# A two-block transformer kernel: four modulation blocks moved from the first routing into the second layer's mixing, the entry's loads reordered and paired, and the expert loads' queue bound to program order

## The chip, the cores and the metric

The kernel runs on one core of a Trainium2 chip. The metric is the device time of one execution in microseconds (us). The kernel before takes 2650.71 us, the median of three runs (2647.95 to 2651.56). The execution that was profiled took 2657.17 us, of which the trace spans 2655.0 us.

Engines are called PE (matrix engine; PEld is its weight load), DVE (vector), ACT (scalar), POOL (GpSimd) and SP (the queue from which nearly all loads are issued; SPq in the trace).

## The reference

A first block of two layers, then a second block. One layer of the first block works on 512 tokens `x` and 256 context tokens `xc`:

```
mods  = silu(c) @ ada_w[i] + ada_b[i]           # 1024 x 6144, split in six: shift, scale, gate, twice
cmods = silu(c_ctx) @ ada_w[i] + ada_b[i]
h  = rms_norm(x, n1) * (1 + sc1) + sh1          # hc the same from xc
a_b, a_c, a_h, b_v, b_g, c_q, c_k, c_v, d_q, d_k, d_v = split_proj(h @ w_in)
x  = x + g1 * (concat(conv a, conv b, window attention c, global attention d) @ w_out)
h2 = rms_norm(x, n2) * (1 + sc2) + sh2
aff = softmax(h2 @ router);  gates, idx = top_k(aff.T, cap)     # 16 experts choose their tokens
y  = (silu(xs @ w_gate[e]) * (xs @ w_up[e])) @ w_down[e]        # for each expert, 1024 x 1024 weights
x  = x + g2 * scatter_add(idx, gates * y)
```

In the second layer only `x` goes on (64 tokens for each expert; in the first layer 64 of `x` and 32 of `xc`). The second block (gated delta rule, dilated attention and a gated feed-forward) isn't touched by the change. Everything is float32; the dense products split weights and activations in a high and a low part.

## The kernel before, in words

The stages follow one another: entry (token loads, their norm sums, the first modulation blocks), the first layer's mixing, its routing, its 16 experts, the same for the second layer, then the second block. Each engine executes its instructions in one order, which is fixed when the program is built: a scheduler places them, and each engine waits on semaphores where data or a buffer isn't ready. SP is such a queue too: a load that waits for its buffer holds up every load behind it.

**Buffers for weights.** `raw_tile` (L187) takes one of the five 512 KB buffers of the pool `wp` (tile `raw`). They serve everything in turn: the columns of `w_in` and `w_out` (`colload`, L487, `colload2`, L493), the quarters of the modulation blocks (`ada_load`, L196) and, in the experts, five of the 25 buffers through which the expert weights rotate. The others there are 18 of `rawA` and 2 of `rawB` (in the second layer 20 and 8). `wload` (L1055) loads one tile of 128 x 1024 after the other, in the order in which PE uses them: g0, u0, g1, d0, u1, g2, d1, ... d15, eight tiles each, 384 in a layer; tile i goes to slot i % 25, where slots 18 to 22 are the five `raw`. A tile's buffer is free again when PE has read it (L1243 for `x`, L1248 for `xc`; in the second layer L1237).

**Modulation.** `ada_gen` (L309) makes a block of 512 modulation columns from four quarter tiles: 16 matrix products (L318), a copy on ACT (L323), four transposes (L327), a sum and a bias on DVE (L329, L330). After the products of a block it may already load the first three quarters of the next one (L320). In the first layer's mixing it makes blocks 4 to 11 of layer 0 and 0 to 7 of layer 1. After block 7 of layer 1 the line

```
if 3 < b < 11 or (l == 1 and b != 7 and b < 11):
    ada_load(l, b + 1, hfs=range(4 if l == 1 and b > 7 else 3))
```

holds by its first half, so the first three quarters of block 8 of layer 1 are loaded there. Blocks 8 to 11 of layer 1 are made in the first layer's routing (L1090, with `steps(ga, 2)` at L1120 and L1152).

**Entry.** Small rows of vectors, the tokens and eight quarters of blocks are issued in turn by SP. The unit `c_q` takes two strips of 64 columns (`pre0[1]`, L272). All four blocks 0, 2, 1, 3 of layer 0 are made before the norm of the tokens (`norm1_first`, L385: for eight column tiles k the high part `hh` on ACT, L396, and the low part `hl` on DVE and POOL, L397, L398). `dense` (L420) runs the units of `w_in`: `wh` on ACT (L442), `wl` on POOL (L443), then 24 products (L473, L475).

**Routing.** Router logits (L1095), softmax (Exp at L1107), eight rounds of top-8 on DVE (L1146 to L1149), the normalised tokens to memory (`hd`, L1132), zeros to the two tables of sums (L1138), a gather of each expert's tokens (L1209), their transposes (L1221), and the first expert's products (L1243).

Of the kernel before, what the change touches and what calls it, by code (L numbers as in the profile page):

```python
# [10 lines left out]
F32 = mybir.dt.float32  # L11
# [123 lines left out]
def main_kernel(ctx, tc, I, out, stop=None, dbg=None, manual=False):  # L135
# [37 lines left out]
    dx = pool(ctx, "dx", space=DRAM).tile([128, 8 * 768], F32)  # L173
# [44 lines left out]
    rows = ent.tile([128, 4, 128], F32)  # L218
    xin = xip.tile([128, 4, 1024], F32)
    cin = xip.tile([128, 2, 1024], F32)  # L220
    ada0 = ent.tile([128, 4, 4, 1024], F32)
# [20 lines left out]
    x_load(1)  # L242
    row_load(G, 0, "qn", I["q_norm_g"], 2, dup=True)
    row_load(G, 0, "kn", I["k_norm_g"], 2, dup=True)
    row_load(G, 0, "cbb", I["conv_b_b"].rearrange("l (h p) -> (l h) p", p=128), 4)
    row_load(G, 0, "lng", I["conv_ln_g"].rearrange("l (h p) -> (l h) p", p=128), 4)
    row_load(G, 0, "lnb", I["conv_ln_b"].rearrange("l (h p) -> (l h) p", p=128), 4)
# [3 lines left out]
    x_load(2)  # L251
    SY.dma_start(sinkb, bass.AP(tensor=I["sink"].tensor, offset=I["sink"].offset, ap=[[0, 128], [1, 8]]))
    row_load(SY, 0, "fg", I["final_g"].rearrange("(k p) -> k p", p=128), 8)
    row_load(SY, 0, "ln1", I["ln1_2"].rearrange("l (k p) -> (l k) p", p=128), 8)
    x_load(3)
# [6 lines left out]
    ada_load(0, 0, ada0[:, 0], hfs=(2, 3))  # L262
    ada_load(0, 2, ada0[:, 2])
    for t in range(2):
        SY.dma_start(cin[:, t, :], I["ctx"][0, t * 128:(t + 1) * 128, :])
    ada_load(0, 1, ada0[:, 1])
    pre0 = {}
    pre0[0] = raw_tile().rearrange("p (k c) -> p k c", k=8)
    SY.dma_start(pre0[0], I["w_in"][0, :, 1536:1664].rearrange("(k p) c -> p k c", p=128))
    pre0[1] = raw_tile().rearrange("p (k c) -> p k c", k=8)  # L270
# [3 lines left out]
    ada_load(0, 3, ada0[:, 3])  # L274
# [34 lines left out]
    def ada_gen(l, blocks, pl, psp):  # L309
        g, o, n = RO["adab"]  # L310
        for b in blocks:
# [8 lines left out]
            if 3 < b < 11 or (l == 1 and b != 7 and b < 11):  # L320
                ada_load(l, b + 1, hfs=range(4 if l == 1 and b > 7 else 3))
# [10 lines left out]
            yield  # L332

# [7 lines left out]
    if True:  # L341
        with ExitStack() as e0:
# [4 lines left out]
            def rows_to_cols(g, n):  # L347
                p = pse.tile([128, 512], F32, name="rc")
                T.transpose(p[:, :n], rows[0:n, g, :], ident[0:n, 0:n])
                V.tensor_copy(cols[:, g, 0:n], p[:, :n])  # L350

            rows_to_cols(0, 16)
            A.activation(s2[:, :, 0], col("c"), AF.Silu)
            A.activation(s2[:, :, 1], col("cc"), AF.Silu)
            ga = ada_gen(0, (0, 2, 1, 3), sqp, pse)
            ss = ent.tile([128, 6], F32)
            for t in range(6):
# [16 lines left out]
                if t == 1:  # L374
                    rows_to_cols(1, RO["n", 1])
# [4 lines left out]
            for g in (0, 2, 3):  # L380
                rows_to_cols(g, RO["n", g])
            V.tensor_scalar(nsink, sinkb, -1.0, None, op0=OP.mult)

        entry.close()

        def norm1_first(sqp):
            a1 = sqp.tile([128, 8, 2], F32, name="a1")
            for k in range(8):
# [32 lines left out]
        def dense(units, hh, hl, dw, dps, la=3, pre={}, ahead=None):  # L421
# [5 lines left out]
            def load(i):  # L427
                if i in pre:
                    raw[i] = pre[i]
                elif i < len(units):  # L430
                    raw[i] = raw_tile().rearrange("p (k c) -> p k c", k=8)
                    units[i][0](raw[i])

            def split(i):
                if i < len(units):
                    nk = units[i][4] if len(units[i]) > 3 else 8
                    hi[i] = []
                    for a in range(0, nk, 4):
# [3 lines left out]
                        A.activation(wh[:, :n], raw[i][:, a:a + n], AF.Copy)  # L442
                        G.tensor_tensor(wl[:, :n], raw[i][:, a:a + n], wh[:, :n].bitcast(F32), op=OP.subtract)  # L443
# [41 lines left out]
        def colload(src, c0, n=128):  # L485
            def f(raw):
                SY.dma_start(raw[:, :, 0:n], src[:, c0:c0 + n].rearrange("(k p) c -> p k c", p=128))  # L487
            return f

        def colload2(src, ca, cb):  # L490
            def f(raw):
                for h, c in enumerate((ca, cb)):
# [529 lines left out]
        def experts(l, rwpA, lg, rbias, a2, nA, nB):  # L1022
# [37 lines left out]
            if has:  # L1060
                ada_load(1, 8)
# [918 lines left out]
```

## Time and profile before

| stage | from, us | to, us |
|---|---|---|
| entry, to the first full pace of the units | 0 | 65 |
| first layer's mixing | 65 | 456 |
| its routing | 456 | 502 |
| its experts | 502 | 1057 |
| second layer's norm, mixing and routing | 1057 | 1389 |
| its experts | 1389 | 1868 |
| second block | 1868 | 2655 |

| | us |
|---|---|
| median of three runs | 2650.71 |
| profiled execution | 2657.17 |
| its span in the trace | 2655.0 |
| PE busy | 2476.4 (93%) |
| DVE, ACT, POOL busy | 1092.9, 870.2, 637.8 |

The span is the time from the first to the last instruction of the trace. PE is busy nearly all of the time, so a stage ends when PE is through with it, save where PE waits: in the entry, in routing, and in parts of the second layer. In the experts' stages the DMA engines are busy throughout as well.

### The profile page before, as it was taken

Reading aid. Unit: us, or ns where it says so; the run is one execution under the profiler, and the core shown is the slowest. Engines: PE = TensorE matmul, PEld = TensorE weight load, DVE = VectorE, ACT = ScalarE, POOL = GpSimd, SP = SyncE. Lnnn points to the kernel's source line nnn. Section 1 sums busy time; section 2 is a strip of 40 time slices with the busy share of each in tenths; the row PEclk is TensorE's granted clock in tenths of the full one; section 3 lists DMA queues with packets and bytes.
Section 4 is the critical chain, followed back from the end, with each engine's and each line's share of the span. In section 5 each row is a group of like instructions: output and inputs, shape, how many; then the busy total and the mean of one; then the engine's idle time right before and its main releaser. Section 6 shows DMA issues by size and latency. Waiting matters only on the chain.

```text
span 2655.0 us, 41308 instructions
## 1 busy us (share of the span) xinstructions
PE 2476.4 (93%) x16415; PEld 1500.4 (57%) x16415; DVE 1092.9 (41%) x2371; ACT 870.2 (33%) x1769; POOL 637.8 (24%) x552
## 2 busy tenths in 40 slices
PE   7999999699999999899979989898899999999998
PEld 4766777344444333577753322132577787888886
DVE  4488852311111113689641102021665555444411
ACT  4544362211111110464531111110562435443422
POOL 3533112011111100633220000000333233444443
PEclk8999999899999999799989999999899999999999
DMA  8454455999999998222179999999421102333332
GB/s 281 140 165 139 149 177 197 322 383 385 385 386 385 388 394 313 58 59 52 61 289 386 394 398 399 399 404 409 130 67 32 40 25 64 95 96 96 92 96 67
DMA packets 324758, 584.08 MB, mean 220 GB/s; under 512 B 36864, under 2 KB 190007, under 8 KB 323927
## 3 DMA queue, kind: packets, MB, share of 16 engines
q1 hardware_dynamic: 311943, 555.16, 57.7%
q0 software_dynamic: 12480, 26.23, 4.1%
q8 instruction: 129, 2.11, 0.3%
q14 instruction: 62, 0.51, 0.1%
q10 hardware_dynamic: 144, 0.08, 0.0%
HBM read 556.74 MB, written 18.87 MB: 217 GB/s over the span
## 4 chain that ended last, share of the span: by engine, by line
PE 62%; DMA 21%; DVE 9%; issue 3%; POOL 2%; ACT 1%; SPq 1%; ACTq 0%; DVEq 0%; POOLq 0%
PE px L473 21%; DMA rawA<-in_w_gate_dram 4%; DMA rawA<-in_w_down_dram 4%; PE ax L1243 3%; DMA rawA<-in_w_up_dram 3%; PE yx L1243 3%; PE ux L1243 3%; PE g L473 2%; PE s L553 2%; PE y L584 2%; PE px L475 2%; DMA rawB<-in_w_gate_dram 2%; PE pt L565 2%; PE ac L1248 2%; PE pt L473 2%
## 5 line engine op out<-in xcount | busy, mean ns | idle before, releaser
L443 POOL TENSOR_TENSOR wl<-raw,wh 128x512 fp32r<-128x512 f32 (+1 forms) x312 | 408.2, 1311 | 962.0 <-ACT wh L442 768.1
L442 ACT ACTIVATE wh<-raw 128x512 fp32r<-128x512 f32 (+1 forms) x312 | 193.6, 625 | 441.2 <-PE px L473 211.0
L473 PE MATMUL px<-hh,wh 128*128 128x512 f32 x768 | 315.7, 412 | 6.4 <-DVE xT L1401 1.8
L473 PE MATMUL px<-hh,wl 128*128 128x512 f32 x768 | 313.1, 408 | 6.6 <-POOL wl L443 6.6
L473 PE MATMUL px<-hl,wh 128*128 128x512 f32 x768 | 314.6, 410 | 3.8 <-DVE hl L1019 1.9
L1225 ACT ACTIVATE xt<-tr,mod,a 128x64 f32<-128x64 f32 x256 | 86.9, 405 | 295.5 <-PE tr L1221 285.1
L473 PEld LDWEIGHTS px<-hh,wh 128*128 128x128 f32 x768 | 148.7, 194 | 41.2 <-issue 6.1
L473 PEld LDWEIGHTS px<-hh,wl 128*128 128x128 f32 x768 | 148.8, 194 | 39.7 <-POOL wl L443 7.3
L473 PEld LDWEIGHTS px<-hl,wh 128*128 128x128 f32 x768 | 148.7, 194 | 37.5 <-issue 3.8
L1369 DVE SCALAR_TENSOR_TENSOR Yx<-yx,gcol,Yx 64x512 fp32r<-64x512 f32 x36 | 27.0, 750 | 268.7 <-ACT Yx L1368 268.7
L1209 POOL DMA_INDIRECT xg<-hd,gidx x32 | 29.7, 927 | 431.9 <-PE tr L1221 398.3
L785 DVE SCALAR_TENSOR_TENSOR yT<-ub,cols,yT 128x512 f32<-128x512 f32 (+1 forms) x180 | 126.5, 718 | 0.6
L1243 PE MATMUL ax<-rawA,xt 128*32 128x512 f32 x856 | 116.8, 597 | 2.2 <-DMA rawA<-in_w_gate_dram 2.1
L1273 ACT ACTIVATE sa<-ax 128x512 f32<-128x512 f32 x32 | 19.1, 597 | 290.9 <-PE ax L1243 183.1
L1300 POOL DMA_INDIRECT sumx<-ys,place x14 | 22.0, 1571 | 376.5 <-ACT ys L1347 376.5
L1243 PE MATMUL ux<-rawA,xt 128*32 128x512 f32 x800 | 106.1, 594 | 0.1
L1237 PE MATMUL ux<-rawA,xt 128*64 128x512 f32 x328 | 87.3, 611 | 8.1 <-DMA rawA<-in_w_up_dram 8.0
L1237 PE MATMUL yx<-rawA,hT 128*64 128x512 f32 x316 | 81.5, 621 | 11.0 <-DMA rawA<-in_w_down_dram 10.0
L565 PE MATMUL pt<-tab,P 128*128 128x128 f32 x448 | 82.2, 284 | 6.8 <-DVE PT L571 4.3
L1368 ACT ACTIVATE Yx<-yx,gcol 64x512 fp32r<-64x512 f32 x36 | 24.6, 682 | 190.7 <-PE yx L1237 138.4
L1228 DVE TENSOR_SCALAR xt<-tr,a,mod 128x32 f32<-128x32 f32 x128 | 39.0, 310 | 115.0 <-ACT xt L1225 114.5
L1237 PE MATMUL ax<-rawA,xt 128*64 128x512 f32 x316 | 77.7, 612 | 7.6 <-DMA rawA<-in_w_gate_dram 7.2
(593 smaller groups left out, 4895.0 us busy)
## 6 DMA issues: line engine op xcount, KB each, us to landing
rawA<-in_w_gate_dram SPq DMA_DIRECT2D x186, 512.0 KB, 10.4
rawA<-in_w_up_dram SPq DMA_DIRECT2D x182, 512.0 KB, 10.2
rawA<-in_w_down_dram SPq DMA_DIRECT2D x151, 512.0 KB, 10.4
raw<-in_ada_w_dram SPq DMA_DIRECT2D x80, 512.0 KB, 5.7
raw<-in_w_down_dram SPq DMA_DIRECT2D x74, 512.0 KB, 10.2
raw<-in_w_gate_dram SPq DMA_DIRECT2D x62, 512.0 KB, 8.1
raw<-in_w_in_dram SPq DMA_DIRECT2D x56, 512.0 KB, 3.9
raw<-in_w_up_dram SPq DMA_DIRECT2D x55, 512.0 KB, 10.2
```

The source lines that it names most:

```text
L442: A.activation(wh[:, :n], raw[i][:, a:a + n], AF.Copy)
L443: G.tensor_tensor(wl[:, :n], raw[i][:, a:a + n], wh[:, :n].bitcast(F32), op=OP.subtract)
L473: T.matmul(px, lhsT=w[:, k % 4, :], rhs=h[:, k0 + k, 0:512], start=st, stop=sp_)
L475: T.matmul(pc, lhsT=w[:, k % 4, :], rhs=h[:, k0 + k, 512:nt], start=st, stop=sp_)
L553: T.matmul(s[:, :w], lhsT=q, rhs=k, start=(a == 0), stop=(a == len(mm) - 1))
L565: T.transpose(pt[:, (t - a) * 128:(t - a + 1) * 128], P[:, t * 128:(t + 1) * 128], ident)
L584: T.matmul(y[64 * g:64 * g + 64, bi * 128:(bi + 1) * 128], lhsT=vs[g][t], rhs=PTs[i, g][t // 4][:, (t % 4) * 128:(t % 4 + 1) * 128], start ...
L785: V.scalar_tensor_tensor(acc[:, j, o:o + n], src, w, acc[:, j, o:o + n], op0=OP.mult, op1=OP.add)
L1225: A.activation(xt[:, kk, 0:64], p[:, k * NX:k * NX + 64], AF.Identity, bias=M[l][:, 24 + kk, 0:1], scale=a2[:, kk, 0:1])
L1237: T.matmul(px[64 * g:64 * g + 64, :], lhsT=lx(u), rhs=w[:, 512 * hf:512 * hf + 512], start=first, stop=last)
L1243: T.matmul(px[32 * g:32 * g + 32, :], lhsT=lx(u)[:, 32 * (g % 2):32 * (g % 2) + 32], rhs=w[:, 512 * hf:512 * hf + 512], start=first, stop= ...
L1248: T.matmul(pc[32 * g:32 * g + 32, :], lhsT=lc(u), rhs=w[:, 256 * q:256 * q + 256], start=first, stop=last)
```

## The change

Five things are changed. (1) The loads of the entry are issued in another order: tokens first, then blocks 0 and 2, the context, the first unit's columns, blocks 1 and 3, and the small rows last; two units that need neighbouring strips of 64 columns are loaded as one pair of tiles of 256 columns (`pair_load`), in all of the mixing. (2) Only blocks 0 and 2 of layer 0 are made before the norm; the norm is made in two halves of four column tiles, and blocks 1 and 3 come between them. (3) Blocks 8 to 11 of layer 1 are no longer made in the first layer's routing but in the second layer's mixing; the load of the first three quarters of block 8 after block 7 stays where it was. (4) The tables of sums are zeroed in the first mixing and not in routing. (5) The experts' loop runs under `manual_schedule` for SP: SP's instructions there keep the order of the program. The sums of the last expert are loaded and added in another order.

```diff
-    ada_load(0, 0, ada0[:, 0], hfs=(0, 1))
...
+    for t in range(1, 4):
+        x_load(t)
+    ada_load(0, 0, ada0[0])
+    ada_load(0, 2, ada0[2])
+    for t in range(2):
+        SY.dma_start(cin[:, t, :], I["ctx"][0, t * 128:(t + 1) * 128, :])
+    pre0 = {0: raw_tile().rearrange("p (k c) -> p k c", k=8)}
+    SY.dma_start(pre0[0], I["w_in"][0, :, 1536:1664].rearrange("(k p) c -> p k c", p=128))
+    ada_load(0, 1, ada0[1])
+    ada_load(0, 3, ada0[3])
+    def pair_load(src, c0):
+        ts = [raw_tile(), raw_tile()]
+        for i, t in enumerate(ts):
+            SY.dma_start(t.rearrange("p (k c) -> p k c", k=4),
+                         src[512 * i:512 * i + 512, c0:c0 + 256].rearrange("(k p) c -> p k c", p=128))
+        return ts
+    pre0[1] = pre0[2] = pair_load(I["w_in"][0], 1280)
...
-    for h in range(2):
-        SY.dma_start(pre0[1][:, :, 64 * h:64 * h + 64],
-                     I["w_in"][0, :, 1280 + 128 * h:1344 + 128 * h].rearrange("(k p) c -> p k c", p=128))
...
             if 3 < b < 11 or (l == 1 and b != 7 and b < 11):
-                ada_load(l, b + 1, hfs=range(4 if l == 1 and b > 7 else 3))
+                ada_load(l, b + 1, hfs=range(3))
...
-            ga = ada_gen(0, (0, 2, 1, 3), sqp, pse)
+            ga = ada_gen(0, (0, 2), sqp, pse)
...
+                    norm1_first(range(4), a1)
+                    gd = dense(units, hh, hl, dw, psp, pre=pre0, ahead=4)
+                    next(gd)
+                    drain(ada_gen(0, (1, 3), sqp, psp))
+                    norm1_first(range(4, 8), a1)
...
                     def ada_rest():
                         yield from ada_gen(0, range(4, 12), sqp, psp)
                         yield from ada_gen(1, range(0, 8), sqp, psp)
                     ga = ada_rest()
+                else:
+                    ga = ada_gen(1, range(8, 12), sqp, psp)
...
+                    zz = sqp.tile([128, 512], F32, name="sq")
+                    G.memset(zz, 0.0)
+                    for acc_, n in zip(accs, (8, 4)):
+                        SY.dma_start(acc_.rearrange("(p a) c -> p (a c)", p=128).rearrange("p (b c) -> p b c", c=512),
+                                     zz[:, None, :].to_broadcast([128, n, 512]))
...
             wload(nA if has else nA + 5)
-            if has:
-                ada_load(1, 8)
...
-                    ga = ada_gen(1, range(8, 12), mp, Psum(ps, {"yx": 1}, {"misc": "yx"})) if has else iter(())
...
+                with tc.manual_schedule(engines={mybir.EngineType.SP}):
+                    gather(0)
+                    gather(1)
+                    xpose(0)
+                    for e in range(17):
```

Below, a row names the line, the operation and what it writes and reads; the numbers behind a tile's name tell its uses apart. First PE in the first layer's routing and at the first expert's start. Before:

```order
L1161 MATMUL tr_4734<-tab_70,tg_4724 128x80
L1162 MATMUL tr_4734<-tab_70,ti_4725 128x80
L318 MATMUL yx_4672<-raw_4649,s2_74 32x512 x2
L318 MATMUL yx_4672<-raw_4651,s2_74 32x512 x2
L1221 MATMUL tr_4795<-tab_70,xg_4790 128x96 x4
L1221 MATMUL tr_4808<-tab_70,xg_4790 128x96
L318 MATMUL yx_4672<-raw_4653,s2_74 32x512 x2
L1221 MATMUL tr_4808<-tab_70,xg_4790 128x96 x3
L1243 MATMUL ax_4821<-rawA_4384,xt_4794 32x512 x4
```

The same place after:

```order
L1173 MATMUL tr_4639<-tab_72,tg_4629 128x80
L1174 MATMUL tr_4639<-tab_72,ti_4630 128x80
L1233 MATMUL tr_4702<-tab_72,xg_4697 128x96 x4
L1233 MATMUL tr_4715<-tab_72,xg_4697 128x96 x4
L1255 MATMUL ax_4728<-rawA_4393,xt_4701 32x512 x4
L1260 MATMUL ac_4729<-rawA_4393,xt_4701 32x256 x4
```

The products of the modulation blocks that stood ahead of the first expert's transposes are gone from there.

PE in the second layer's mixing after, where `kC` and `qC` are the window attention's keys and queries:

```order
L560 MATMUL s_10085<-kC_9788,qC_9786 128x256 x2
L560 MATMUL s_10088<-kC_9788,qC_9786 128x256 x2
L326 MATMUL misc_10105<-raw_3681,s2_76 32x512 x2
L326 MATMUL misc_10105<-raw_3683,s2_76 32x512 x2
L326 MATMUL misc_10105<-raw_3685,s2_76 32x512 x2
L326 MATMUL misc_10105<-raw_10103,s2_76 32x512 x2
L560 MATMUL s_10122<-kC_9788,qC_9786 128x256 x2
```

Block 8 of layer 1 now stands here. Its first three quarters carry numbers from the first layer's mixing (`raw_3681` to `raw_3685`), its last one a number from this place.

SP at the start of the first layer's experts. Before, quarters of modulation blocks (`in_ada_w`) stand among the expert tiles, and three gate tiles in `raw` buffers right behind them:

```order
L196 DMA raw_4653<-in_ada_w_dram 128x2x512
L196 DMA raw_4655<-in_ada_w_dram 128x2x512
L196 DMA raw_4681<-in_ada_w_dram 128x2x512
L196 DMA raw_4683<-in_ada_w_dram 128x2x512
L196 DMA raw_4685<-in_ada_w_dram 128x2x512
L1055 DMA rawA_4831<-in_w_down_dram 128x1024
L196 DMA raw_4687<-in_ada_w_dram 128x2x512
L1055 DMA raw_4752<-in_w_gate_dram 128x1024
L1055 DMA raw_4754<-in_w_gate_dram 128x1024
L1055 DMA raw_4756<-in_w_gate_dram 128x1024
```

After:

```order
L1083 DMA rawA_4900<-in_w_up_dram 128x1024
L1083 DMA rawA_4910<-in_w_up_dram 128x1024
L1083 DMA rawA_4920<-in_w_gate_dram 128x1024
L1083 DMA rawA_4936<-in_w_gate_dram 128x1024
L1083 DMA raw_4657<-in_w_gate_dram 128x1024
L1083 DMA raw_4659<-in_w_gate_dram 128x1024
L1083 DMA rawA_4946<-in_w_gate_dram 128x1024
L1083 DMA raw_4661<-in_w_gate_dram 128x1024
L1083 DMA raw_4956<-in_w_gate_dram 128x1024
L1083 DMA raw_4966<-in_w_gate_dram 128x1024
L1083 DMA raw_4987<-in_w_gate_dram 128x1024
L1083 DMA raw_4997<-in_w_gate_dram 128x1024
```

`raw_4657`, `raw_4659` and `raw_4661` are the gate tiles 20, 21 and 22 of the 384; they now stand behind the loads of tiles 25 and on.

The entry on SP, before (`ada_89` holds all four blocks):

```order
L196 DMA ada_89<-in_ada_w_dram 128x2x512 x6
L265 DMA cin<-in_ctx_dram 128x1024 x2
L196 DMA ada_89<-in_ada_w_dram 128x2x512 x4
L269 DMA raw<-in_w_in_dram 128x8x128
L272 DMA raw<-in_w_in_dram 128x8x64 x2
L196 DMA ada_89<-in_ada_w_dram 128x2x512 x4
```

And after (`ada_96`, `ada_97`, `ada_94` and `ada_95` are blocks 0, 2, 1 and 3):

```order
L239 DMA xin<-in_x_dram 128x1024 x3
L199 DMA ada_96<-in_ada_w_dram 128x2x512 x4
L199 DMA ada_97<-in_ada_w_dram 128x2x512 x4
L252 DMA cin<-in_ctx_dram 128x1024 x2
L254 DMA raw<-in_w_in_dram 128x8x128
L199 DMA ada_94<-in_ada_w_dram 128x2x512 x4
L199 DMA ada_95<-in_ada_w_dram 128x2x512 x4
L262 DMA raw<-in_w_in_dram 128x4x256 x2
```

The two loads of 64-column strips have left the place ahead of the last block.

## Rows read from the trace of the kernel before

**Rows 1.** Busy time of the engines in four stretches, the granted clock, DMA

```profile
core 0: us, PE busy (x) PEld busy (x) DVE busy (x) ACT busy (x) POOL busy (x), PEclk, DMA share, GB/s
456.00:502.00 46.00, 26.11 (x154) 12.35 (x153) 25.21 (x107) 13.82 (x22) 4.52 (x28) 0.78 0.79 281
502.00:1057.00 555.00, 548.20 (x6427) 221.12 (x6430) 97.38 (x264) 77.87 (x189) 57.27 (x46) 1.00 1.01 377
1100.00:1320.00 220.00, 201.25 (x1215) 157.53 (x1215) 173.90 (x390) 120.59 (x272) 86.69 (x73) 0.95 0.22 56
1500.00:1600.00 100.00, 89.01 (x367) 25.56 (x367) 15.95 (x24) 13.52 (x33) 2.66 (x3) 0.98 1.03 398
```

**Rows 2.** Timeline of ACT, one row an expert: start us, us, operation [idle <-releaser]

```profile
520.80 0.60 ACT L1273 ACTIVATE sa<-ax 128x512 f32<-128x512 f32 x1
...
837.66 0.60 ACT L1273 ACTIVATE sa<-ax 128x512 f32<-128x512 f32 x1 [13.37 <-PE ax L1243]
...
871.39 0.60 ACT L1273 ACTIVATE sa<-ax 128x512 f32<-128x512 f32 x1 [14.25 <-PE ax L1243]
...
1012.89 0.60 ACT L1273 ACTIVATE sa<-ax 128x512 f32<-128x512 f32 x1 [19.68 <-PE ax L1243]
```

**Rows 3.** What SP's queue waited for, 500 to 1060: us, times, longest

```profile
SPq L1055 <- DMA rawA<-in_w_gate_dram: 112.6, 97, 2.9
...
SPq L1055 <- PE uc L1248: 13.9, 28, 1.8
```

**Rows 4.** Chain of waits, 440 to 520: start us, us, what

```profile
463.40 3.60 DMA raw<-in_ada_w_dram
...
480.82 15.39 DMA raw<-in_ada_w_dram
```

**Rows 5.** The page's DMA issues: KB each, median us to landing

```profile
rawA<-in_w_gate_dram SPq DMA_DIRECT2D x186, 512.0 KB, 10.4
...
raw<-in_ada_w_dram SPq DMA_DIRECT2D x80, 512.0 KB, 5.7
```

**Rows 6.** Timeline in the first layer's routing

```profile
463.29 0.26 DVE L1106 TENSOR_TENSOR af<-af,mx 128x96 f32<-128x96 f32 x1
...
464.32 0.60 ACT L323 ACTIVATE sq<-yx 128x512 f32<-128x512 f32 x1 [2.99 <-PE yx L318]
464.93 1.28 ACT L1107 ACT_TABLE_LOAD   x1
466.23 0.28 ACT L1107 ACTIVATE af<-af 128x96 f32<-128x96 f32 x1
...
485.02 1.00 POOL L1209 DMA_INDIRECT xg<-hd,gidx  x1 [6.65 <-DVE tA L1191]
...
496.26 3.44 PE L318 MATMUL yx<-raw,s 128*32 128x512 f32 x8 [14.04 <-DMA raw<-in_ada_w_dram]
...
502.24 1.07 PE L1243 MATMUL ax<-rawA,xt 128*32 128x512 f32 x8
```

**Rows 7.** Chain of waits in the second layer's routing

```profile
1384.05 4.07 DMA xg<-hd,gidx
...
1389.46 2.76 PE ax L1237 x5
```

**Rows 8.** Chain of waits in the entry

```profile
24.78 5.11 SPq L272
29.93 4.29 SPq L272
...
36.24 6.55 DMA ada<-in_ada_w_dram
...
48.54 0.82 ACT hh L396
...
50.89 0.87 DVE xin L397
...
52.69 0.88 DVE xin L397
...
63.97 1.11 POOL hl L398
```

**Rows 9.** Timeline: POOL's low parts; a modulation block on PE in the first mixing

```profile
72.97 4.63 POOL L443 TENSOR_TENSOR wl<-raw,wh 128x512 fp32r<-128x512 f32 x3
...
110.58 0.60 PE L327 MATMUL misc<-tab,sq 128*128 128x128 f32 x4
...
118.80 1.92 PE L318 MATMUL misc<-raw,s 128*32 128x512 f32 x16
```

More of the change, by code (lines that the diff above doesn't have):

```diff
@@ L172, in main_kernel @@
     xcT = xp.tile([128, 8, 256], F32)
-    dx = pool(ctx, "dx", space=DRAM).tile([128, 8 * 768], F32)
+    dxp = pool(ctx, "dx", space=DRAM)
+    dx = dxp.tile([128, 8 * 768], F32)
+    accs = dxp.tile([1024, 512], F32, name="sumx"), dxp.tile([1024, 256], F32, name="sumc")
     stA = cst.tile([128, 768], F32)
@@ L217, in main_kernel @@
     ent = pool(entry, "ent", side="right")
-    rows = ent.tile([128, 4, 128], F32)
+    rows = raw_tile()[:, 0:512].rearrange("p (g c) -> p g c", g=4)
     xin = xip.tile([128, 4, 1024], F32)
     cin = xip.tile([128, 2, 1024], F32)
-    ada0 = ent.tile([128, 4, 4, 1024], F32)
+    entry2 = ExitStack()
+    ada0 = {b: pl.tile([128, 4, 1024], F32, name=f"ada{b}")
+            for pl, bs in ((ent, (1, 3)), (pool(entry2, "ent2", side="right"), (0, 2))) for b in bs}
     def row_load(eng, g, name, ap, n, dup=False):
@@ L332, in ada_gen, with rows_to_cols @@
             yield
+    def rows_to_cols(psp, name, g, n):
+        p = psp.tile([128, 512], F32, name=name)
+        T.transpose(p[:, :n], rows[0:n, g, :], ident[0:n, 0:n])
+        V.tensor_copy(cols[:, g, 0:n], p[:, :n])
     es_l0 = ExitStack()
@@ L379, in main_kernel, with norm1_first @@
             drain(ga)
[L380 to L388, printed above, removed]
+        entry2.close()
+        def norm1_first(ks, a1):
+            for k in ks:
                 if k % 4 == 0:
@@ L429, in load @@
                     raw[i] = pre[i]
+                elif i < len(units) and len(units[i]) == 6 and units[i][5]:
+                    raw[i] = raw[i - 1]
+                elif i < len(units) and len(units[i]) == 6:
+                    raw[i] = units[i][0]()
                 elif i < len(units):
@@ L487, in f @@
                 SY.dma_start(raw[:, :, 0:n], src[:, c0:c0 + n].rearrange("(k p) c -> p k c", p=128))
[L488 to L492, printed above, removed]
-                    SY.dma_start(raw[:, :, 64 * h:64 * h + 64], src[:, c:c + 64].rearrange("(k p) c -> p k c", p=128))
             return f
@@ L615, in layer @@
                 psp = Psum(ps, {"px": 3, "s": 2, "pt": 1, "misc": 1, "y": 1}, {"pc": "px"})
+                c0 = dict(a_b=0, a_c=256, a_h=512, b_v=768, b_g=1024, c_q=1280, c_k=1536, c_v=1664,
+                          d_q=1792, d_k=2048, d_v=2176)
+                evs = []
+                units = []
+                for n in "c_k c_q c_v b_g b_v d_k d_q d_v a_c a_h a_b".split():
+                    for j in range(2 if n[2] == "q" or n[0] in "ab" else 1):
+                        nt, ev = NT if n[2] == "q" or n[0] in "ab" else 768, partial(lambda i, px, pc: evs[i](px, pc), len(units))
+                        if n[2] == "q":
+                            units.append((partial(pair_load, w_in, c0[n]), ev, nt, 0, 8, j))
+                        else:
+                            units.append((colload(w_in, c0[n] + 128 * j), ev, nt))
                 if has:
                     hh, hl = hh0, hl0
-                    norm1_first(sqp)
+                    a1 = cst.tile([128, 8, 2], F32)
+                    norm1_first(range(4), a1)
[3 more added lines that the diff above has]
+                    norm1_first(range(4, 8), a1)
+                    entry.close()
                     xip_es.close()
@@ L1119, in experts @@
                     V.tensor_copy(D[:NP], pd[:NP, 0:256])
-                    for _ in steps(ga, 2):
-                        pass
                     wload(6 if l else 0)
@@ L1149, in experts @@
                             V.match_replace(out=D[:NP], in_to_replace=v8, in_values=D[:NP], imm_value=-1.0)
-                        if i in (2, 4, 6):
-                            for _ in steps(ga, 2):
-                                pass
                     tg = hp.tile([80, 128], F32)
@@ L1266, in run_gu @@
                         if each and u % 2:
-                            each(8 + u // 2)
+                            each(u)
                     acc[w, e] = (px, pc)
@@ L1341, in down @@
                         wload(1)
-                        if has and e == 15:
-                            sums_add(u)
+                        if has and e == 15 and u % 2:
+                            sums_add(4 + u // 2)
                     if has and e < 14:
```

133 lines of the change are left out of this document (55 added, 78 removed).

## The prediction, made before the changed kernel ran

> **What bounds the kernel now.** I read the busy time by stage first, then the timeline of one instruction that occurs once an expert, then what SP's queue waits for, and last the chain of waits in the two places where PE stands still. In the first layer's experts PE is busy 548.20 of 555.00 us, but the DMA engines are full too (share 1.01, 377 GB/s) [rows 1]. The activation after an expert's gate products marks the pace: from 520.80 to 837.66 there are ten steps, the first of 16 tiles (u0, g1) and the others of 24, so 232 tiles in 316.86 us, 1.37 a tile, with PE as the limit; the last four steps take 1012.89 - 871.39 = 141.50, 1.47 a tile, with the loads as the limit [rows 2]. PE waits for almost nothing there since each load is issued 25 tiles ahead of its use: SP's queue waits long in total for earlier transfers (112.6 us on the gate tiles) and little for PE (13.9 us on `uc`) [rows 3]. So the reserve of buffers is what hides the loads. A load alone takes 3.60 us to land [rows 4]; in the full queue the median is 10.4 us [rows 5].
>
> PE stands still in routing (26.11 of 46.00 us busy, granted clock 0.78) [rows 1]. There the chain waits 15.39 us for modulation quarters [rows 4], and PE's own idle ahead of that block is 14.04 us [rows 6]. In the entry SP spends 5.11 and 4.29 us on issuing the two strips of 64 columns, ahead of the last block's load [rows 8].
>
> **The change part by part.** Entry. The two strips leave the queue ahead of the last block: 5.11 + 4.29 = 9.4 us earlier, if the chain's next step, the landing of that block (6.55), follows as before [rows 8]. Only four column tiles of the norm are left after the last block instead of eight: a column tile costs DVE 52.69 - 50.89 = 1.8 us [rows 8], so 4 x 1.8 = 7.2 us less. Against that, block 3's transposes now stand on PE behind the first products of the pair's unit; the pair is loaded last, so a load (3.60) [rows 4] and a low part on POOL (4.63 / 3 = 1.54) [rows 9] come into the chain, of which some 0.6 lies beside block 3's products: +4.5. Together -12 us. Bounds: 0, if POOL's last low part at 63.97 [rows 8] only shifts against other waits, and -20, if the pair lands in time.
>
> Routing. The four blocks go. ACT's copy at 464.32 stood ahead of the table load and the Exp at 466.23, whose input was ready at 463.29 + 0.26 = 463.55 [rows 6]: 2.7 us earlier, and all top-8 rounds with it. The gather is issued at 485.02 - 2.7 = 482.3 and takes 1.0 [rows 6]; from the gather's transfer to the first product the second layer, which has no blocks there, shows 1389.46 - 1384.05 = 5.4 us [rows 7]. So the first product comes at 489 instead of 502.24 [rows 6]: -13 us. Bounds -10 and -15.
>
> First layer's experts. Here the change costs. The line that loads ahead after block 7 still fetches three quarters of block 8 in the first mixing, but they are read in the second layer's mixing. So three of the five `raw` buffers are held through all of these experts, and the five `raw` places of every 25 tiles share two. In the program of the changed kernel the load of tile 20 of a cycle waits for PE's products on tile 18, that of tile 22 for tile 20, and SP, in program order, holds the 20 loads behind them back. Reserve gone, a cycle goes like this, from the end of tile 18 at t: load 20 is issued and lands at t + 0.15 + 3.60 (a load alone, since the queue has run dry) [rows 4]; PE reaches the end of tile 20 at t + 5.12 with 1.37 a tile [rows 2]; load 22 lands at t + 8.87; 21 more tiles up to tile 18 of the next cycle arrive behind it at the pace r of a full queue, and PE needs 1.37 for the last. So a cycle is C = 10.24 + 21 r. The pace is 512 KB over 398 GB/s = 1.32 at the best stretch [rows 1] and 1.47 at the slowest [rows 2]; with 1.40 (377 GB/s in this stage [rows 1] gives 1.39) C = 39.6; I take 40 for the two loads' issue. Before, a cycle cost 555 / 384 x 25 = 36.1. The first such wait that isn't covered by what was loaded earlier: tile 43 ends at 489 + 44 x 1.37 + 3.5 (two for a cold PE, 1.5 for the first, partly covered waits) = 553, so load 45 goes out at 553 and load 47 at 558. Thirteen cycles on, load 372 is issued at 558 + 13 x 40 = 1078 and lands at 1082. The 12 tiles then left take half of what the last 24 took before, (1057 - 1012.89) / 2 = 22 [rows 1, 2]: end at 1104. The stage lasts 1104 - 489 = 615 instead of 555: +60 us. Bounds: C = 38 (r = 1.32) gives +34; C = 42 (r = 1.47 with a landing of 4.1) gives +86.
>
> [...]
>
> Second layer's mixing. Four blocks come in: 1.92 + 0.60 = 2.5 us of PE each [rows 9], 10 in all. In that stretch PE is idle 220.00 - 201.25 = 18.75 us [rows 1], and some of it will take a block in. At its start only two `raw` buffers are free for the unit columns as well. +6 us, between 0 and +14. The second layer's experts have all five buffers again and the same order: 0.
>
> The zeroing, the small rows and the new order of the last sums: 0. They lie beside the mixing, where PE sets the pace, or beside experts that now wait for loads; the bounds are -2 and +3, since PE's wait on sums was short.
>
> **Sum.** -12 - 13 + 60 + 6 = +41. The profiled execution of 2657.17 becomes 2698; it lay 6.46 us above the median of 2650.71, so the median becomes 2692.
>
> **Rivals.** Only the gains: the two lone waits in a cycle are hidden, because the loads were the limit in the last third of the stage anyway [rows 2] and a cycle stays at its 36.1. Then -12 - 13 + 6 = -19, a median of 2632. For it speaks the DMA share of 1.01; against it that a queue with two places runs dry, so that DMA loses the time too. The point from which it decides: gains of 12 + 13 - 6 = 19 over 13 cycles are 1.5 us a cycle, so a cycle under 36.1 + 1.5 = 37.6 makes the kernel faster. Chance 0.05.
>
> Loads land later: if a load alone takes the 5.7 us of the modulation quarters' median [rows 5] and the pace is 1.47, C = 45.3, 5.3 more, +69: 2761. For it speaks that these loads come right behind a busy stretch; against it that the queue is empty by then. Chance 0.08.
>
> The granted clock falls in the gaps: at 0.78, as in routing with its gaps [rows 1], 21 tiles need 36.9 instead of 28.8 and C is about 48, +104: 2796. Against it, the second layer's experts hold 0.98 with PE busy 89.01 of 100 us [rows 1]. Chance 0.04.
>
> The entry's gain fails, since PE takes block 1's products ahead of the first unit and these wait for its load: +12, 2704, within the forecast's range. Chance 0.10.
>
> **How the numbers follow.** The forecast has 0.73, to which the entry's rival is added for the sign. The range 2660 to 2730 takes in C from 38 to 42.4 with the entry's and the mixing's ends, and leaves 2632 and most of 2761 and 2796 out. A difference under 0.2% (5.3 us) can't be told from no change with this kernel. Faster: 0.05, the first rival. Same: 0.03, C near 37.6. Slower: 0.92.
>
> **What would show it.** Right: in the first experts PE waits about 2.4 us twice in every 25 tiles for a tile in `raw`, SP's queue waits for PE (products on `raw`) where it waited for transfers, the mean DMA rate of the stage falls to about 340 GB/s, and the activations stand 38 to 39 us apart in the mean (24 of 25 tiles of 40). The first product stands at about 477 (489 less the entry's 12), and routing has no load of modulation quarters. Wrong: a stage of 555 us with PE as busy as before, a wait in it for something else, or a second layer's mixing longer by more than 14.

## The result and the profile after

The changed kernel takes 2776.24 us (median of four runs, 2767.27 to 2779.97) against 2651.14 of the kernel before on the same chip: a ratio of 1.0465, 95% interval 1.0433 to 1.0496. I had forecast slower, 2692 us, and missed the size by two thirds of the loss. The profiled execution's span is 2778.2 us, 123.2 more than before.

From one landmark to the next, read from the first and last products of the routers and experts:

| stretch | before, us | after, us | difference | forecast |
|---|---|---|---|---|
| start to the first router product after the mixing | 460.9 | 455.2 | -5.7 | -12 |
| from there to the first expert's first product | 41.3 | 27.7 | -13.6 | -13 |
| first layer's experts | 555.0 | 687.3 | +132.3 | +60 |
| norm, mixing and routing of the second layer | 332.3 | 342.7 | +10.4 | +6 |
| second layer's experts | 478.7 | 478.6 | -0.1 | 0 |

All of the loss lies in the first layer's experts, and 72 of the 82 us by which the differences were missed; the entry has 6 of the others, the second layer's mixing 4. The busy time by stretch of the kernel after, as in [rows 1] (the same columns; the first row ends at the first expert's product, the second is its experts' stage, the third lies in the second layer's mixing, the fourth in its experts):

```profile
452.00:483.00 31.00, 15.95 (x95) 11.84 (x93) 23.37 (x100) 11.96 (x20) 2.47 (x3) 0.71 0.44 159
483.00:1170.00 687.00, 599.57 (x6400) 208.68 (x6400) 98.70 (x262) 78.04 (x188) 57.39 (x46) 0.97 0.82 299
1220.00:1440.00 220.00, 201.21 (x1248) 152.27 (x1248) 171.62 (x390) 119.13 (x270) 81.02 (x68) 0.96 0.33 92
1610.00:1710.00 100.00, 87.58 (x364) 24.69 (x360) 15.96 (x24) 13.52 (x33) 2.66 (x3) 1.00 1.03 399
```

In the experts the DMA share falls from 1.01 to 0.82 and 377 GB/s to 299: the engines that were full now stand still nearly a fifth of the time. PE is busy 599.57 us instead of 548.20 with no more products (6400 records against 6427), and the granted clock is 0.97 in the mean. What PE waited for in that stage (columns as in [rows 3]; before, all waits for expert tiles were 2.1 us):

```profile
PE yx L1255 <- DMA raw<-in_w_down_dram: 36.5, 20, 3.1
PE ux L1255 <- DMA raw<-in_w_up_dram: 15.8, 8, 3.1
PE ux L1255 <- DMA rawA<-in_w_up_dram: 14.5, 22, 1.1
PE ax L1255 <- DMA raw<-in_w_gate_dram: 10.3, 7, 3.3
...
PE ax L1255 <- DMA rawA<-in_w_gate_dram: 3.0, 5, 0.8
PE ux L1255 <- DMA rawB<-in_w_up_dram: 2.1, 3, 1.0
PE yx L1255 <- DMA rawA<-in_w_down_dram: 1.7, 2, 1.3
```

The three lines of `raw` are 62.6 us in 35 waits. The forecast's lone loads (loads issued into a queue that has run dry), two in each of thirteen cycles, come to nearly the same, 2 x 2.4 x 13 = 62, but in 26 waits: that the sums agree so closely is in part chance. The other lines, with one of 0.8 us that isn't shown, are 22 us for tiles of `rawA` and `rawB`, which have buffers enough: I had none of those. SP's queue, the answer to [rows 3], waited 79.1 us for PE (`ac`) and 59.7 (`yc`), where it had waited 13.9 (`uc`).

One cycle on PE (start us, us, operation, [idle <-releaser]):

```profile
817.21 1.04 PE L1255 MATMUL yx<-raw,hT 128*32 128x512 f32 x8
821.66 1.07 PE L1255 MATMUL yx<-raw,hT 128*32 128x512 f32 x8 [2.98 <-DMA raw<-in_w_down_dram]
...
826.82 1.06 PE L1255 MATMUL yx<-raw,hT 128*32 128x512 f32 x8 [2.21 <-DMA raw<-in_w_down_dram]
...
830.20 1.07 PE L1255 MATMUL yx<-rawB,hT 128*32 128x512 f32 x8 [0.58 <-DMA rawB<-in_w_down_dram]
...
843.02 1.06 PE L1255 MATMUL ux<-rawA,xt 128*32 128x512 f32 x8 [0.58 <-DMA rawA<-in_w_up_dram]
844.44 1.07 PE L1255 MATMUL ax<-rawA,xt 128*32 128x512 f32 x8
845.87 0.44 PE L1302 MATMUL tr<-tab,sa 128*128 128x128 f32 x2
846.24 1.07 PE L1255 MATMUL ax<-rawA,xt 128*32 128x512 f32 x8
847.67 0.33 PE L1302 MATMUL tr<-tab,sa 128*128 128x128 f32 x1
847.92 1.07 PE L1255 MATMUL ax<-rawA,xt 128*32 128x512 f32 x8
...
861.27 1.04 PE L1255 MATMUL yx<-raw,hT 128*32 128x512 f32 x8
...
866.79 1.22 PE L1255 MATMUL yx<-raw,hT 128*32 128x512 f32 x8 [2.76 <-DMA raw<-in_w_down_dram]
```

From 821.66 to 866.79 is one cycle of 25 tiles: 45.1 us, forecast 40. It is a typical one: from the wait that ends at 562.26 (tile 47) to the one that ends at 1148.01 (tile 372), thirteen cycles take 45.06 us each. The two lone loads stand as forecast: tile 20 waited for at 821.66, tile 22 at 826.82, 5.16 us apart (forecast 5.12). Then eleven tiles up to 844.44 take 17.6 us, 1.60 each, with short waits; and then a transpose or two stands behind each gate tile and the first two down tiles, which makes 1.66 to 1.80 us of a tile's 1.29 (844.44 to 846.24, 846.24 to 847.92). From tile 22 at 826.82 to tile 18 of the next cycle at 861.27 PE takes 34.45 us for 21 tiles, 1.64 each: the forecast's "21 r" had 1.40.

The DMA engines in the same cycle (columns as in [rows 1]):

```profile
826.00:829.00 3.00, 2.18 (x24) 0.70 (x28) 0.00 (x0) 0.00 (x0) 0.00 (x0) 1.00 1.00 392
826.00:856.00 30.00, 26.73 (x297) 8.79 (x297) 2.62 (x5) 0.69 (x1) 3.12 (x2) 1.00 1.03 391
847.00:850.00 3.00, 3.00 (x34) 0.99 (x30) 0.28 (x1) 0.00 (x0) 0.00 (x0) 1.00 1.03 407
856.00:859.00 3.00, 3.00 (x35) 1.04 (x31) 0.70 (x3) 1.86 (x5) 0.00 (x0) 1.00 0.21 79
859.00:862.00 3.00, 3.00 (x38) 1.14 (x34) 1.16 (x4) 1.58 (x4) 0.94 (x1) 1.00 0.07 8
```

They are full until 856 (the second row: 391 GB/s in the mean, so 1.34 us for a tile of 512 KB, as good a pace as the forecast had), then almost idle for 6 us while PE works on: everything that SP may issue has been issued, and the next load waits for PE. And the landing of loads behind a gap, from the chain of waits four cycles earlier (start us, us):

```profile
639.58 3.22 DMA raw<-in_w_gate_dram
...
648.54 9.84 DMA rawA<-in_w_up_dram
658.40 13.13 DMA rawA<-in_w_gate_dram
```

A lone load lands after 3.22 us ([rows 4] had 3.60, for the first of three issued within 1.41 us); those issued behind it take 9.84 and 13.13, as in the full queue of [rows 5]. The Trainium skill's DMA: Bandwidth & Descriptors, on the anatomy of one DMA, has a fit for DMAs issued from GpSimd, about 2.0 us plus the bytes at 436 GB/s; for 512 KB that gives an estimate of 3.2 us. These loads are issued from SP; the lone one's 3.22 agrees with it, the ones in a queue don't.

Routing, the answer to [rows 6]: the gather's transfer at 476.47 and the first product at 482.92, 6.45 us later, with no wait for modulation quarters:

```profile
476.47 4.81 DMA xg<-hd,gidx
481.41 1.51 PE tr L1233 x8
482.92 1.87 PE ax L1255 x8
```

### The profile page after: what moved, and what is told of

The parts are those of the page before. It is cut to its first block, busy times and chain, and to the rows that moved or that the text cites. A ratio compares the mean times of both kernels' runs of the same rounds, so it can differ in the third digit from the quotient of the medians.

```text
span 2778.2 us, 40987 instructions
## 1 busy us (share of the span) xinstructions
PE 2521.0 (91%) x16415; PEld 1488.8 (54%) x16415; DVE 1097.6 (40%) x2371; ACT 870.9 (31%) x1769; POOL 631.9 (23%) x545
## 4 chain that ended last, share of the span: by engine, by line
PE 61%; DMA 25%; DVE 8%; POOL 2%; issue 2%; ACT 1%; SPq 1%; ACTq 0%; DVEq 0%; POOLq 0%
PE px L486 20%; DMA rawA<-in_w_up_dram 6%; DMA rawA<-in_w_down_dram 4%; PE ax L1255 4%; DMA rawA<-in_w_gate_dram 3%; PE yx L1255 2%; PE g L486 2%; PE y L591 2%; PE s L560 2%; PE px L488 2%; PE ac L1260 2%; PE ux L1255 2%; DMA raw<-in_w_down_dram 2%; PE pt L572 2%; DMA rawB<-in_w_gate_dram 2%
## 5 line engine op out<-in xcount | busy, mean ns | idle before, releaser
L1221 POOL DMA_INDIRECT xg<-hd,gidx x32 | 29.4, 918 | 657.0 <-PE tr L1233 605.7
L1293 DVE TENSOR_TENSOR sa<-ux,sa 128x512 f32<-128x512 f32 x32 | 22.1, 692 | 269.8 <-PE ux L1255 173.3
```

## The experiments

Theory A: the three held quarters leave two buffers for five places of the rotation, and with SP in program order the reserve of every load falls as low as 2 tiles. Rivals: B, the binding of SP by itself; D and G, the missing buffers or the mean reserve, and not the least one; E, what stands on PE matters or doesn't. All stages are from profiles, first product to last product of the first layer's experts. The reserve is counted in the program: how many tiles behind the tile that PE must have read does the load stand. Each stage is read from one profile.

**No buffer held.**

```diff
-            if 3 < b < 11 or (l == 1 and b != 7 and b < 11):
+            if (3 < b < 11 and (l, b) != (1, 7)) or (l == 1 and b != 7 and b < 11):
```

> The changed kernel, with block 8 of the second layer not loaded ahead in the first mixing, so that no raw buffer is held through the first layer's experts; SP stays in program order. Theory A (two lone loads in every 25 tiles, because five raw places share two buffers): every load again goes out 25 tiles ahead, the first experts' stage falls from 687 us to 555, and only the other stages' differences stay (-6 entry and mixing, -14 routing, +6 to +10 second mixing): 2637 to 2642 us. Rival B (binding SP to program order is what costs): the stage stays near 687, 2770 us. Rival C (the loads of the pairs and blocks elsewhere cost): over 2700.

Measured: 2628.5 us, ratio 0.989 (0.987 to 0.991). Stage 541.5 us; the DMA engines are full again:

```profile
485.00:1027.00 542.00, 537.38 (x6407) 219.95 (x6405) 97.12 (x262) 76.41 (x190) 57.34 (x46) 0.99 1.02 379
```

B and C fall. The stage is even 13.5 us shorter than before, which I had not expected. This one line makes the change faster than the kernel before.

**Held, but 22 places instead of 25.**

```diff
-            slots = ["A"] * nA + ["W"] * 5 + ["B"] * nB
+            slots = ["A"] * nA + ["W"] * (2 if has else 5) + ["B"] * nB
...
-                wload(5 if has else 0)
+                wload(2 if has else 0)
```

> The changed kernel with the three quarters still held, but the rotation of the first layer's expert tiles made of 22 places (18 rawA, 2 raw, 2 rawB) instead of 25. Theory A: what costs is that five places share two buffers, not that three buffers are missing; each load goes out 22 tiles ahead, more than enough for 10 us of landing, the stage takes 555 to 560, total 2640 to 2648. Rival D (fewer buffers cost in themselves, since the loads are the limit there): at least half of the 132 us stays, over 2700.

Measured: 2639.61 us, 0.9936 (0.9913 to 0.9959), stage 551.3. D falls: three buffers less cost 10 us, not 146, and in the last sixth of this stage the transposes stand between the tiles, which by their price below is likely a part of the 10.

**Held, five places on two buffers, but apart from each other.**

```diff
+            slots = list("AAAAW" * 3 + "AAAW" * 2 + "BB") if has else ["A"] * nA + ["W"] * 5 + ["B"] * nB
```

> The changed kernel with the three quarters still held and still five raw places in 25 sharing two buffers, but the five places stand apart in the rotation (4 rawA, raw, three times; 3 rawA, raw, twice; 2 rawB) instead of side by side. The mean reserve of the loads stays 12 tiles as in the changed kernel, the least becomes 8 instead of 2. Theory A (it is the least reserve against the landing of a load in the queue, up to 10.4 us or 7.6 tiles, that decides): PE waits for no raw tile, the stage is 555 plus at most 40 for the interleaved transposes, total 2640 to 2680. Rival G (held buffers, or the mean reserve, set the cost): the stage stays near 687, 2776.

Measured: 2659.34 us, 1.0013 (0.9996 to 1.003), stage 568.7. PE's waits for expert tiles are 5.4 us:

```profile
PE ax L1255 <- DMA rawA<-in_w_gate_dram: 2.6, 3, 2.0
PE ux L1255 <- DMA rawA<-in_w_up_dram: 1.6, 3, 0.7
PE ax L1255 <- DMA raw<-in_w_gate_dram: 1.2, 2, 0.9
```

The same two buffers and the same mean reserve (some 12 tiles) as in the changed kernel, 119 us less of stage. G falls.

**The same, three places apart.** (`"AAAAAAAAAA" + "WAA" * 4 + "WBB"`)

> As spread10, but the raw places stand only three apart (10 rawA, then raw with two rawA four times, raw with two rawB): the mean reserve is 12 tiles again, the least 6, that is 8.2 us. Theory A: less than the 10.4 us of a load in a full queue, so PE waits some 2 us once or twice a cycle, less than with 4 (617 us in hold1) and more than with 8: stage 590 to 615, 2676 to 2700. Rival G: 2776, as the mean reserve is the same.

Measured: 2678.74 us, 1.0088 (1.0058 to 1.0118), stage 585.5, waits 14.6: a little better than expected.

**One quarter held instead of three.**

```diff
-                ada_load(l, b + 1, hfs=range(3))
+                ada_load(l, b + 1, hfs=range(1 if (l, b) == (1, 7) else 3))
```

> The changed kernel with one quarter of block 8 held instead of three. The loads of the experts' raw tiles go out 4 tiles ahead at the least instead of 2, and PE's transposes stay interleaved. Theory A: 4 tiles x 1.37 = 5.5 us are more than a lone load's 3.75, so PE no longer waits for it; only the transposes are left (at most 3 us a cycle, 40), partly within the loads' own pace: stage 555 to 595, 2642 to 2682, and PE's waits for raw tiles are gone from the trace. Rival F (cost in proportion to the buffers held): 132 / 3 = 44, stage 599, 2686, with waits for raw tiles in each cycle.

Measured: 2706.09 us, 1.0191 (1.0169 to 1.0213), stage 616.7: above both expectations. The waits for `raw` are nearly gone (2.8 us), as A had it, but of the 34.6 us of waits 31.8 are for tiles behind them, so a landing of 3.75 wasn't the measure for those.

**Transposes in groups.** SP and PE in program order; one line, on top of the changed kernel, and below of spread10, hold1 and hold_w3:

```diff
-                with tc.manual_schedule(engines={mybir.EngineType.SP}):
+                with tc.manual_schedule(engines={mybir.EngineType.SP, mybir.EngineType.PE}):
```

> The changed kernel with PE as well as SP in program order in the first experts: the transposes stand in groups again (4 and 2 behind the fourth gate tile, 8 behind the fourth up tile) and not one or two behind each gate tile; the held buffers and the order of the loads stay. Theory A': of the 5 us a cycle by which I was short, the interleaved transposes are 3 (ten tiles at 1.70 instead of 1.37), as the next lone load can go out only when PE is through with them: 13 cycles x 3 = 40 us less than the changed kernel, 2736. Rival E: the loads behind the gap limit anyway, and the transposes lie in waits: no change, 2776.

Measured: 2762.28 us, 1.0397 (1.0377 to 1.0418), stage 673.9. Between the two: 13.4 us, not 40. Waits rose from 84.7 to 99.0, so more than half of what the transposes cost is taken back by the loads:

```profile
PE yx L1255 <- DMA raw<-in_w_down_dram: 29.4, 22, 2.2
PE ax L1255 <- DMA rawA<-in_w_gate_dram: 21.7, 16, 2.7
PE ux L1255 <- DMA raw<-in_w_up_dram: 16.8, 11, 3.2
PE ax L1255 <- DMA raw<-in_w_gate_dram: 13.3, 8, 4.5
```

> As spread10, with PE also in program order in the first experts, so that the transposes stand in groups. Theory A: with no waits for loads the transposes count in full, so the stage falls to 545 to 560, total 2632 to 2648, and the difference to spread10 is the price of interleaved transposes (up to 40 us). Rival E: the loads limit here too and there is no difference to spread10.

Measured: 2653.34 us, 0.9995 (0.9979 to 1.0011), stage 561.2, just above the 545 to 560 of theory A: 7.5 less than spread10, and again waits rose (5.4 to 17.2). In the times the two can't be told apart, their intervals overlap.

> hold1 (one quarter held, least reserve 4) with PE in program order too, so that the transposes stand in groups. By the account of hold1's stage (541.5 of free, 31 us more of waits for expert tiles, 3 us of low clock, 41 us left for the interleaved transposes) the stage falls from 617 towards 576; waits take some of it back, as in the changed kernel, where 13 of 687 were won: 576 to 600, 2666 to 2690. Rival: the 41 us are something else (the DMA engines), and the stage stays at 610 or more.

Measured: 2689.09 us, 1.0141 (1.0112 to 1.017), stage 598.8, as expected: 17.9 less than hold1, waits 45.9.

**Three places on two buffers.** 23 places (`["W"] * (3 if has else 5)`, `wload(3 if has else 0)`), the three quarters held.

> The changed kernel, three quarters held, with a rotation of 23 places (18 rawA, 3 raw, 2 rawB): three raw places share two buffers, so there is one lone load in 23 tiles instead of two in 25, with a least reserve of 2. By my prediction's formula (lone waits, then the loads at 1.40 a tile with PE right behind) a cycle would take 5.12 + 20 x 1.40 = 33.1, no more than before, stage 545 to 560, 2640 to 2650. Theory A'' (behind a gap eight loads are under way at once, the next ten tiles come at 1.6 a tile, PE can't make that up, and then the DMA engines stand still until PE is through): 3 to 4 us a cycle more, 15 cycles, stage 590 to 615, 2680 to 2705.

Measured: 2732.64 us, 1.0293 (1.0275 to 1.0312), stage 644.2. Both expectations missed, the formula of the prediction by 84 us at its upper end. Waits are 57.9 us, the clock lower (0.98 in the mean, 0.50 behind a wait of 4.16 us at 814), and the DMA engines stand idle at the end of each cycle as in the changed kernel.

> hold_w3 (three raw places on two buffers, one lone load in 23 tiles) with PE in program order. By its account (541.5, 54 more of waits, 9 of low clock, 40 left for transposes) the stage falls from 644 to between 604 (nothing taken back) and 630, 2693 to 2718. Rival: 644, 2732, if PE only waits longer instead.

Measured: 2717.0 us, 1.0246 (1.0212 to 1.028), stage 624.0, as expected: 20.2 less.

**Held, SP not bound.**

```diff
-                with tc.manual_schedule(engines={mybir.EngineType.SP}):
+                if True:
```

> The changed kernel, three quarters held, without binding SP to program order: loads for rawA and rawB pass the waiting raw loads and keep 20 to 29 tiles of reserve, and only the raw tiles come 2 tiles ahead. Theory A: the DMA engines need not stand still, but three raw loads a cycle still land after PE wants them, 2 to 3 us each and more behind other loads: 13 cycles x 4 to 9 us, stage 595 to 660, 2690 to 2760. Rival H: with the others far ahead, the waits are all that is lost and PE's other work fills them: stage below 580, 2675; then it is the binding that makes the held buffers cost 132 us.

Measured: 2693.2 us, 1.0156 (1.0123 to 1.019), stage 599.8, within theory A's range and above rival H's, waits for expert tiles 39.2. The DMA engines hardly stand still (400 us in the middle of the stage):

```profile
600.00:1000.00 400.00, 374.94 (x4361) 157.34 (x4357) 55.45 (x146) 49.77 (x125) 43.49 (x33) 0.99 0.98 358
```

So of the stage's 146 us over free, 87 need the binding together with the held buffers. Some of the 87 are transposes, which stand in groups here: against hold_pe, bound and grouped as well, it is 74.

**Not held, SP not bound.** The same edit on free.

> The kernel free without the binding of SP to program order in the experts. The loads of the first experts keep their order and their reserve of 25 tiles either way. Theory A: the binding costs and gives nothing there, stage 541.5 as in free, total within 3 us. Rival B': the 13.5 us by which the stage of free is shorter than that of before (541.5 against 555.0) come from the binding: then this kernel is about 13 us slower than free; otherwise they come from the quarters of modulation blocks that no longer share the DMA engines with the first expert loads.

> The kernel free once more, as the partner of free_z_again on the same chip: 0.989 of before.

Measured on one chip: free_nosp 0.991 (0.9896 to 0.9923), stage 540.4; free_again 0.9895 (0.988 to 0.991), stage 540.2. With all buffers the binding costs and gives nothing in that stage. So the 13.5 us that free has over before there come from elsewhere. The two traces show where they lie: 5.7 us ahead of the first activation `sa` (18.6 us behind the first product before, 12.9 in free), where the kernel before has 20 products of the moved blocks on PE among the first expert's; 6.5 behind the last `sa` (44.3 against 37.8), where the last expert's sums are added in another order and PE no longer waits 2.1 us for one of them; 1.3 on the way between. So the blocks that left explain less than half, and more by their products on PE than by their loads (PE waited 1.1 us for one). Neither part was tried by itself.

**Zeros later.** The block with `zz` moved in front of the last `run_all` of the first mixing, on free.

> The kernel without held buffers (free), and the zeros to the tables of sums (3 MB) written before the last part of the first mixing instead of its beginning. Theory Z: in the changed kernel these writes share the DMA engines with the small moves of the rotary units at 62 to 82 us, which land after 5.7 us in the median instead of 2.4, PE stands still and its granted clock falls to the lower level (0.53) from 82 to 96 us; here that goes away, 6 to 10 us less than free: 2619 to 2623 on a chip with free at 2628.5, or 0.984 to 0.986 of before instead of 0.989. Rival Y: the small moves wait for the modulation quarters' loads instead, and nothing changes: 0.989.

> The kernel free_z beside free on one chip. Two profiles differ by 10 us (2621.7 and 2631.8 of span, with the first expert's product 13 us earlier), while the ratios on two chips were the same, 0.989. Theory Z: 6 to 10 us less than free on the same chip. Rival Y': within 3 us of free, and the difference of the profiles was chance.

Measured: 0.9889 (0.9869 to 0.9909), and beside free (0.9895) on one chip 0.9892 (0.9876 to 0.9908). In the traces the first expert's product comes 13 and 7 us earlier; in the times the difference is 0.03% of before, well within the intervals. The 6 to 10 us that theory Z expected aren't there, the rival's "within 3 us" fits, and a gain of a few us is not settled.

The runs in one table, sorted by the least reserve. Waits are PE's for expert tiles; clock is the share of the stage lost to it, worked out as (1 - mean granted clock) x stage from the stage's row, to some 3 us; the rest is the stage less both. The column on transposes says whether they stand in groups or one or two between tiles.

| kernel | least reserve, tiles | transposes | stage | waits | clock | rest |
|---|---|---|---|---|---|---|
| after | 2 | between | 687 | 85 | 21 | 581 |
| hold_pe | 2 | grouped | 674 | 99 | 20 | 555 |
| hold_w3 | 2, once a cycle | between | 644 | 58 | 13 | 573 |
| hold_w3_pe | 2, once a cycle | grouped | 624 | 61 | 19 | 544 |
| hold_nosp | 2, `raw` alone | grouped or mixed | 600 | 39 | 12 | 549 |
| hold1 | 4 | between | 617 | 35 | 6 | 576 |
| hold1_pe | 4 | grouped | 599 | 46 | 0 | 553 |
| spread6 | 6 | between | 585 | 15 | 0 | 570 |
| spread10 | 8 | between | 569 | 5 | 0 | 564 |
| spread10_pe | 8 | grouped | 561 | 17 | 0 | 544 |
| hold_22 | 22 | grouped, last sixth between | 551 | 5 | 0 | 546 |
| free | 25 | grouped | 541 | 3 | 5 | 533 |
| before | 25 | grouped, last quarter between | 555 | 2 | 0 | 553 |

In the three pairs at reserve 2 and 4 the transposes between tiles cost 26, 29 and 23 us of rest, in the pair at reserve 8 20. The stage gains less by grouping them (13, 20, 18 and 8), since waits rise.

## Why the prediction was wrong in size

**The mechanism held.** Three held buffers, five places on two, SP blocked behind the waiting load, PE waiting twice in 25 tiles: the program showed it and the trace has it, with 62.6 us of waits for `raw` against 62 by the forecast's steps (so close by some luck, as said). The Trainium skill's Perfetto Trace Analysis (Optimization Strategy) says that the same gap repeating on the engine that should be saturated can mean too little SBUF for the next tile; here it repeats twice in 25 tiles, and free, with three buffers more, has 3.4 us of such waits left.

**The step that failed is the cycle, C = 10.24 + 21 r with r = 1.40.** It let PE go through the 21 tiles behind the second lone load right behind their loads, at the pace of a full queue: 29.4 us. The loads did keep that pace (1.34 us a tile from 826 to 856), but PE didn't: it took 34.45 us, 1.64 a tile, and the next lone load had to wait for it. Of the 5.05 us too little, 2.45 are the four short waits from 830 to 843; most of the others lie where the transposes stand between the tiles. Thirteen cycles of 45.06 instead of 40 are 66 of the 72 us by which the stage was missed; the other 6 are gone by tile 47, read 79 us behind the first product instead of 73. Against before, the stage's +132 us are, by the table, 83 of waits, 21 of low clock, 26 of transposes and 2 of the rest. Of these:

- Waits: 62 foreseen, 22 not. A load behind a gap doesn't land in 3.6 us but in about 10: at some 400 GB/s those are the bytes of seven or eight loads, which are issued close together and share the rate. By this estimate a tile with a reserve under 10 / 1.37 = 7 tiles is late. I had both numbers, 3.60 in [rows 4] and 10.4 in [rows 5], and used only the first. The runs show the edge: waits of 35 us with a least reserve of 4, 15 with 6, 5 with 8.
- Transposes: I took PE's order in the experts for unchanged. It isn't: from 580 us on a transpose or two stands behind most gate tiles and some of the others, 26 us in this stage. The order of the changed kernel showed that before the run. Why the scheduler places them so was not tried.
- The price of this stood in the trace of before as well, and I read it wrongly: the last four steps of [rows 2], 1.47 us a tile, I put down to the loads. But PE is busy there for all but 1.6 of 141.50 us and waits 1.5 us for tiles; from 915 on the transposes stand between the tiles, as they do after (the row is as in [rows 1]):

```profile
871.39:1012.89 141.50, 139.89 (x1604) 52.84 (x1596) 24.16 (x62) 21.85 (x52) 12.53 (x10) 1.00 1.03 391
```

- Clock: a rival with 0.04 in the prediction, at +104 us. It is neither absent nor that large: behind longer waits the granted clock is at the lower of its two levels for some microseconds (in hold_w3 0.50 from 814 to 817, behind a wait of 4.16 us; here 0.63 in the mean from 693.9 to 698, behind one of 3.11, and 1.00 again from 698). Over the stage it is 0.97 in the mean, some 21 us.
- Against this, 13.5 us that free gains in the stage over before were not in the sum either: the products of the moved blocks on PE in the first expert, and the new order of the last sums, which I had set at 0.
- The rival "loads land later" (2761 us, a cycle of 45.3) has the nearest number, but not the reason: its lone load took 5.7 us, the trace's 3.22.

**The end of a cycle.** I had PE reach tile 18 of the next cycle as soon as it lands. In the trace the last load has landed at 856 and PE is there at 862: the DMA engines stand still for the difference in each cycle. That is what the binding adds; without it (hold_nosp) the later loads pass, the DMA share in the middle of the stage is 0.98 and the stage is 87 us shorter (74 with the transposes in groups in both).

**Entry and first mixing, -12 forecast, -5.7 measured.** The entry's steps gave more than forecast: the first product of a unit comes at 33.9 instead of 49.4. Ten of these 15.5 us are lost again between 70 and 107, where I had set the zeroing at nothing. The 3 MB of zeros go out at 61 us, ahead of the rotary units' small moves; one of these takes 7.93 us in the chain, PE waits, and its granted clock is 0.53 from 82 to 96.5, nearly the lower of its two levels (PE was busy 2.58 of the 4 us before; the last row is as in [rows 1]):

```profile
72.07 7.93 DMA qC<-sq
...
82.91 1.22 PE L560 MATMUL s<-kC,qC 128*128 128x256 f32 x4 [2.34 <-DMA qC<-sq]
...
82.00:90.00 8.00, 4.22 (x14) 3.20 (x14) 3.34 (x9) 5.25 (x9) 6.28 (x7) 0.53 0.51 123
```

The landing of these moves has a median of 5.7 us (before 2.4). In free_z, with the zeros later, it is 2.7, where free has 5.8, and the clock from 82 to 96 is 1.00 instead of 0.63: the cause is shown for the moves and the clock, but what it is worth at the end is not, as said above.

**Routing and the second layer** came as worked out: -13.6 for -13; +10.4 for +6, within its bounds of 0 to +14; the experts of the second layer unchanged. The rival "only the gains" (2632 us) is what free shows, 2628.5: its condition, a cycle under 37.6 us, is not met by the changed kernel (45.06) but by free (541.5 / 384 x 25 = 35.3). Its sum is short: it had -19 us, free is 31 and 26 us below the kernel before beside it on two chips, and the stage's 13.5 us make most of the difference.

## What to carry to other kernels

A load that is issued ahead of use holds its buffer until the use: when the use is moved, move the load with it, or count what else rotates through that pool. Compare the least reserve of a queue of loads, in tiles times the time of a tile, with the landing time of a load in the full queue, not with that of a load alone, and not with the mean reserve. Where waits appear, look also at what the build does with the order of the waiting engine.

## What the runs showed of the hardware

Behind a gap the DMA engines were at full rate within 3 us (392 GB/s), and 391 GB/s in the mean of the 30 us that followed; single loads of 512 KB took 9.84 to 13.13 us to land there, a lone one 3.22. Binding a queue to program order cost nothing (540.4 against 540.2 us of stage) with 25 tiles of reserve, and 74 to 87 us with 2. Transposes of one or two between tiles instead of in groups made 1.66 to 1.80 us of a tile's 1.29, 20 to 29 us in a stage of 384 tiles before waits took some of it back.
